# A Conformer-style layer on one core: weight differences on VectorE, and a new order at the start of both FFNs

## The chip, the core and the metric

The kernel runs on one core of a Trainium2 chip, as one launch. A core has TensorE (PE in the profile; its weight loads are PEld), VectorE (DVE), ScalarE (ACT), GpSimd (POOL) and SyncE (SP), each with an instruction queue of its own that it works through in order, and 16 DMA engines. The metric is the device time of the launch in microseconds; the median of several runs counts.

## The reference

One layer over x of 1024 tokens and 1024 channels, all in float32 (D_FF is 2816), and a final RMSNorm:

```python
x = x + 0.5 * _swiglu(_rmsnorm(x, ffn1_norm), ffn1_w_gate, ffn1_w_up, ffn1_w_down)
h = _rmsnorm(x, mix_norm); z = h @ w_in
y_a = _spatial_gating(gelu(z[..., :1024]), ...)      # gMLP, 4 groups
y_b = _mlstm_mixer(z[..., 1024:], ...)               # mLSTM, 4 heads
x = x + concat([y_a, y_b]) @ w_out
x = x + 0.5 * _swiglu(_rmsnorm(x, ffn2_norm), ffn2_w_gate, ffn2_w_up, ffn2_w_down)
out = _rmsnorm(x, final_norm)
# _swiglu(x, g, u, d) = (silu(x @ g) * (x @ u)) @ d
```

## The kernel before

**Layout.** x is held transposed, in two chunks c of 512 tokens, each as eight tiles of 128 channels by 512 tokens. Every matmul that needs float32 accuracy is made of three faster ones: an operand is split in a rounded part hi (a cast on ACT, L198) and a rest lo (a subtraction on DVE, L201), and `mm3` (L132) sums hi x hi, hi x lo and lo x hi.

**Seven products instead of eight.** Both FFN matrix products are done by Strassen's scheme in Winograd's form over 2 x 2 blocks, with seven products M = 1 to 7. The activation side has seven units A11, A12, A22, S1, S2, S3, S4 (`A_OF`, L47), which `h_units` (L213) makes: `first` normalizes chunk 0 and splits A11 and A12, `second` normalizes chunk 1 and makes S1, S2, S4, S3 and A22 in turn. That is 16 DVE instructions for S1 (eight normalizations, four sums, four splits), 8 each for S2, S4 and S3, 4 for A22. The weight side has four products (M = 5, 6, 7, 4) whose weight is a difference of two blocks; the difference is made in place in the raw tile and then split into a unit of one of two rings of four.

**gate_up (L255)** goes over 22 blocks b (gate and up weights of 11 pairs), seven products each. One product is four k tiles times three matmuls, twelve, into a PSUM bank; chains X (M = 1, 6, 7, 4), Z (5, 3) and W (2) share banks. The steps begin with the first three blocks interleaved: M = 1 and M = 2 of blocks 0, 1, 2 (steps 0 to 5), then M = 5, 6, 3, 7, 4 of blocks 0 and 1 (steps 6 to 15), then block 2. The difference (L282 to L291) is on DVE for blocks 0 and 1 and on POOL for the others.

**run (L371)** is the loop over steps: it calls `product(i)`, evacuates, then prepares `weight(i + ahead)`, ahead = 6 in gate_up and 3 in down. With `first=6` the first six evacuations are held back until after product 5, and `then()` (the whole of `second`) is issued ahead of them and ahead of weight 11. In FFN2, `then` is `later2`, which first computes the RMS statistics of chunk 1 (`rstd`, L152: a cast, a subtraction, two matmuls with a matrix of ones, then `rsqrt` with a logarithm and an exponential on ACT and four DVE instructions) and then calls `second`.

**down (L396)** goes product by product (M in the order 2, 1, 5, 6, 3, 7, 4), 11 pairs p each; one step is a split of the streamed activation (au<-as) and of the weight (wu<-wq), and 12 matmuls. `diff` (L433) makes the weight differences on POOL five steps ahead, `fetch` issues the loads eight steps ahead on SP's queue. When a chain ends, `evac` (L470) adds into x (L476) and calls a hook: in FFN1 and in the mixer the hook stores x to DRAM on SP's queue and adds its square to an accumulator; at the end of FFN2, `tail3` squares and accumulates on ACT and DVE, multiplies x by the final norm's gain on ACT (L976), and, once a chunk is complete, computes the statistics, multiplies by them on DVE and, for every third tile, POOL (L982), and stores.

A list scheduler places each engine's instructions when the program is built: the order in the code is the priority, and an instruction whose inputs it takes to be ready may go ahead of one that is not. On the chip each queue then runs in that fixed order.

Of the kernel before, what the change touches and what calls it, by code (L numbers as in the profile page):

```python
# [10 lines left out]
F32 = mybir.dt.float32  # L11
F32R = mybir.dt.float32r
AF = mybir.ActivationFunctionType
# [9 lines left out]
KT = D // P  # L23
# [23 lines left out]
A_OF = {1: "A11", 2: "A12", 3: "S4", 4: "A22", 5: "S1", 6: "S2", 7: "S3"}  # L47
UNITS = ("A11", "A12", "A22", "S1", "S2", "S3", "S4")
GROUPS = ((0, 4), (4, 8), (8, 11))


class Net:
# [97 lines left out]
        return acc  # L150

    def rstd(self, acc, hl, pst, pin=True):  # L152
        nc = self.nc
        hi, lo = hl[:, 0], hl[:, 1]
        nc.scalar.copy(hi, acc)
        nc.vector.tensor_sub(lo, acc, hi.bitcast(F32))
        ps = pst("stat")
        for i, a in enumerate((hi, lo)):
            ins = nc.tensor.matmul(ps, self.ones, a, start=i == 0, stop=i == 1)
            if i == 0 and pin:  # L160
                self.tc.keep_in_program_order(ins)
        return self.rsqrt(ps)

    def squares(self, c):
        nc = self.nc
# [47 lines left out]
    def h_units(self, gcol, r):  # L213
        nc = self.nc
        self.h = {
            u: tuple(self.big.tile([P, 4, T], F32R, tag="b", name=f"{u}{s}") for s in ("h", "l")) for u in UNITS
        }

        def put(u, k, src, eng=None):
            self.split(self.h[u][0][:, k], self.h[u][1][:, k], src, eng)  # L220

        def norm(c, k):
            x = self.x[c][k]
            g = self.cols[:, gcol + k : gcol + k + 1]
            nc.vector.scalar_tensor_tensor(x, x, g, r[c], op0=ALU.mult, op1=ALU.mult)
            return x

        def first():
            for j, u in enumerate(("A11", "A12")):
                for k in range(4):  # L230
                    put(u, k, norm(0, 4 * j + k))

        def second():
            x = self.x
            quads = [(x[0][k], x[0][4 + k], x[1][k], x[1][4 + k]) for k in range(4)]
            for k, (a11, a12, a21, a22) in enumerate(quads):
                norm(1, k)
                norm(1, 4 + k)
                nc.vector.tensor_add(a21, a21, a22)
                put("S1", k, a21)  # L240
            for k, (a11, a12, a21, a22) in enumerate(quads):
                nc.vector.tensor_sub(a21, a21, a11)
                put("S2", k, a21)
            for k, (a11, a12, a21, a22) in enumerate(quads):
                nc.vector.tensor_sub(a12, a12, a21)
                put("S4", k, a12)
            for k, (a11, a12, a21, a22) in enumerate(quads):
                nc.vector.tensor_sub(a21, a22, a21)
                put("S3", k, a21)
            for k, (a11, a12, a21, a22) in enumerate(quads):  # L250
                put("A22", k, a22)

        return first, second

    def gate_up(self, n):  # L255
        nc, d = self.nc, self.d
# [15 lines left out]

        def weight(b, M):
            r0 = row(b, 0)
            eng = nc.vector if b < early - 1 else nc.gpsimd
            if M in (1, 2):
                src = r0[:, M - 1]
            else:
                r1 = row(b, 1)
                if M == 5:  # L280
                    src = r1[:, 0]
                    eng.tensor_sub(src, r1[:, 0], r0[:, 0])  # L282
                elif M == 6:
                    src = r1[:, 0]
                    eng.tensor_sub(src, r1[:, 1], r1[:, 0])  # L285
                elif M == 7:
                    src = r0[:, 0]
                    eng.tensor_sub(src, r1[:, 0], r0[:, 0])
                elif M == 4:
                    src = r0[:, 1]  # L290
                    eng.tensor_sub(src, r0[:, 1], r1[:, 0])  # L291
                else:
                    src = r1[:, 1]
            w = self.unit("wu")
            name = self.split(w[:, 0], w[:, 1], src, after=fence.get("early"))
            if (b, M) == (early - 1, 2):
                fence["early"] = name
            return w
# [69 lines left out]
        steps.append((len(blocks) - 1, 4))  # L368
        return steps, weight, product, evac

    def run(self, steps, weight, product, evac, ahead, first=0, then=None, at=(), early=()):  # L371
        ready = {}
        n = len(steps)
        for what, lead in early:
            for i in range(min(lead, n)):
                what(*steps[i])
        for i in range(min(ahead, n)):
            ready[i] = weight(*steps[i])
        for i, (b, M) in enumerate(steps):
            for what, lead in early:  # L380
                if i + lead < n:
                    what(*steps[i + lead])
            product(b, M, ready.pop(i))
            if i >= first:
                evac(b, M)
            elif i == first - 1:
                then()
                for step in steps[:first]:
                    evac(*step)
            if i + ahead < len(steps):  # L390
                ready[i + ahead] = weight(*steps[i + ahead])
            for when, what in at:
                if when == (b, M):
                    what()

    def down(self, n, xsrc, hook, order, early=None):  # L396
# [36 lines left out]
        def diff(M, p):  # L433
            src = part(p, *source[M])
            if M == 5:
                nc.gpsimd.tensor_sub(src, src, part(p, 0, 0))
            elif M == 6:
                nc.gpsimd.tensor_sub(src, part(p, 1, 1), src)
            elif M == 7:
                nc.gpsimd.tensor_sub(src, part(p, 0, 1), src)  # L440
            elif M == 4:
                nc.gpsimd.tensor_sub(src, src, part(p, 0, 1))

        def units(M, p):
            a = self.unit("au", "u")
# [63 lines left out]
    def weight(self, key, ahead):  # L509
        at = next(i for i, (k, _) in enumerate(self.wq) if k == key)  # L510
        self.prepare(at + 1 + ahead)
        return self.wready[key]
# [376 lines left out]
def layer(ctx, tc, d):  # L889
# [17 lines left out]
    with ExitStack() as f1:  # L907
        net.ffn_pools(f1)
        net.load_x(d["x"])
        r[0] = net.rsqrt(net.squares(0))  # L910
        ps = net.squares(1)
        first, second = net.h_units(0, r)
        first()
        r[1] = net.rsqrt(ps)
        net.run(*net.gate_up(1), ahead=6, first=6, then=second)

        accs = [None, None]
        count = [0, 0]
        h = [None, None]

        def tail(c, k):
            nc.sync.dma_start(x1[c, :, k], net.x[c][k])
            accs[c] = net.square(net.x[c][k], accs[c], net.tmp)
            count[c] += 1
            if c == 0 and count[c] == KT:
                r[0] = net.rstd(accs[0], net.unit("sp"), net.fpsum)

        def early():
            h[0] = net.norm(0, 8, r[0], net.last_mm)

        net.down(1, d["x"], tail, order, ((4, 5), early))

    with ExitStack() as m:
        net.mix_pools(m)
        net.plan_mix()

        def stats1():
            r[1] = net.rstd(accs[1], mixhl(), mixst)

        def rest1():  # L940
            h[1] = net.norm(1, 8, r[1])

        accs2 = [None, None]

        def tail2(c, k):
            nc.sync.dma_start(x2[c, :, k], net.x[c][k])
            accs2[c] = net.square(net.x[c][k], accs2[c], mixsq)

        r2 = [None, None]
        h2 = []  # L950

        def nstats(c):
            r2[c] = net.rstd(accs2[c], mixhl(), mixst)

        def nrest(c):
            h2.extend(net.h_units(16, r2))
            h2[0]()

        net.mix(h, x1, stats1, rest1, tail2, nstats, nrest)

    with ExitStack() as f2:
        net.ffn_pools(f2)

        def later2():
            r2[1] = net.rstd(accs2[1], net.unit("sp"), net.fpsum, False)
            h2[1]()

        net.run(*net.gate_up(2), ahead=6, first=6, then=later2)

        accs3 = [None, None]  # L970
        count3 = [0, 0]

        def tail3(c, k):
            x = net.x[c][k]
            accs3[c] = net.square(x, accs3[c], net.tmp)
            nc.scalar.activation(x, x, AF.Copy, scale=net.cols[:, 24 + k : 25 + k])  # L976
            count3[c] += 1
            if count3[c] == KT:
                rf = net.rstd(accs3[c], net.unit("sp"), net.fpsum)
                for j in range(KT):  # L980
                    o = net.x[c][j]
                    (nc.gpsimd if j % 3 == 2 else nc.vector).tensor_mul(o, o, rf)  # L982
                    (nc.sync if j % 2 else nc.scalar).dma_start(d["out"][c, :, j], o)

        net.down(2, x2, tail3, order)

# [52 lines left out]
```

## Time and profile before

| | |
|---|---|
| median of 3 runs | 1748.37 us (1746.34 to 1748.84) |
| the profiled execution | 1748.65 us, span 1746.9 us |
| mean granted TensorE clock | 0.98 |
| PE busy in the span | 1662.6 us |
| DVE busy | 1108.7 us |
| ACT busy | 688.5 us |
| POOL busy | 447.8 us |

The stages by time in the span: FFN1 from 0 (gate_up to about 450 us, down to about 690), the mixer to 1057, FFN2 to the end (gate_up to about 1496, down to 1727, then the tail). The span goes from the first to the last instruction of the profiled execution; the time of the launch is 1.75 us longer. A row of a timeline gives start and duration in us, the engine and source line, the tile written and the tiles read, and how many alike were merged; in brackets stands how long the engine had been idle and who ended it. The hardware profiler models the ends of matmuls, so two matmuls in a row overlap in the records, and a few records can be missing.

### The profile page before, as it was taken

How to read it: one execution, taken by the hardware profiler on the slowest of the kernel's cores; microseconds unless marked ns; L12 is line 12 of the kernel's file. 1: busy time of each engine (PE TensorE's matmuls, PEld its weight loads, DVE VectorE, ACT ScalarE, POOL GpSimd, SP SyncE). 2: the span in 40 equal slices, each digit the busy share in tenths (PEclk: the TensorE clock that was granted, in tenths of full speed). 3: DMA queues.
4: the chain of work that ended last, by engine and by line, in shares of the span. 5: the costliest groups of instructions: out<-in, count | busy, mean ns of one | idle time of the engine just before them, and what ended most of it. 6: DMA issues, size and time to landing. Idle time of an engine off the chain costs nothing. (4 is left out here: it accounts for less than half of the span.)

```text
span 1746.9 us, 20121 instructions
## 1 busy us (share of the span) xinstructions
PE 1662.6 (95%) x7306; PEld 1347.8 (77%) x7306; DVE 1108.7 (63%) x1524; ACT 688.5 (39%) x1172; POOL 447.8 (26%) x331
## 2 busy tenths in 40 slices
PE   6799999999998999999999997999999999998995
PEld 3678888888886777888877885788888888876874
DVE  7965555555579767842636438955555554589575
ACT  5533333333443345531333324533333333443463
POOL 0133223222139200200304100222332322069000
PEclk9899999999999999999999998999999999999998
DMA  4242332332794232230310433233233331971331
GB/s 157 66 137 94 103 103 97 107 102 88 252 326 139 90 132 72 74 92 12 103 39 12 142 104 115 74 108 103 98 108 113 111 103 62 348 258 67 109 114 49
DMA packets 95701, 200.10 MB, mean 115 GB/s; under 512 B 10473, under 2 KB 14569, under 8 KB 95601
## 3 DMA queue, kind: packets, MB, share of 16 engines
q1 hardware_dynamic: 93712, 195.60, 33.4%
q10 hardware_dynamic: 1888, 3.21, 0.5%
q8 instruction: 57, 0.93, 0.2%
q14 instruction: 44, 0.35, 0.1%
HBM read 145.78 MB, written 52.99 MB: 114 GB/s over the span
## 5 line engine op out<-in xcount | busy, mean ns | idle before, releaser
L201 DVE TENSOR_TENSOR wu<-rg,wu 128x512 fp32r<-128x512 f32 x154 | 133.0, 865 | 128.8 <-ACT wu L198 127.6
L201 DVE TENSOR_TENSOR au<-as,au 128x512 fp32r<-128x512 f32 x154 | 144.5, 939 | 110.0 <-ACT au L198 109.2
L201 DVE TENSOR_TENSOR wu<-ru,wu 128x512 fp32r<-128x512 f32 x154 | 132.9, 864 | 85.7 <-ACT wu L198 84.7
L198 ACT CAST au<-as 128x512 fp32r<-128x512 f32 x154 | 95.7, 622 | 223.5 <-PE pX L138 117.3
L198 ACT CAST wu<-ru 128x512 fp32r<-128x512 f32 x154 | 95.9, 623 | 174.5 <-PE pX L138 53.9
L201 DVE TENSOR_TENSOR wu<-wq,wu 128x512 fp32r<-128x512 f32 x154 | 141.0, 918 | 6.0 <-ACT wu L198 5.9
L138 PE MATMUL pX<-au,wu 128*128 128x512 f32 x352 | 138.6, 394 | 5.6 <-DVE wu L201 5.6
L198 ACT CAST wu<-rg 128x512 fp32r<-128x512 f32 x154 | 95.3, 621 | 109.1 <-PE pZ L138 30.4
L136 PE MATMUL pX<-au,wu 128*128 128x512 f32 x352 | 137.7, 391 | 0.0
L137 PE MATMUL pX<-au,wu 128*128 128x512 f32 x352 | 137.7, 391 | 0.0
L198 ACT CAST wu<-wq 128x512 fp32r<-128x512 f32 x154 | 94.3, 615 | 9.3 <-PE pX L138 4.2
L282 POOL TENSOR_TENSOR rg<-rg,rg 128x512 f32<-128x512 f32 x20 | 26.5, 1326 | 247.7 <-DMA rg<-g 160.2
L138 PEld LDWEIGHTS pX<-au,wu 128*128 128x128 f32 x352 | 66.5, 189 | 22.7 <-DVE wu L201 9.0
L138 PE MATMUL pZ<-au,wu 128*128 128x512 f32 x176 | 71.5, 407 | 9.8 <-DVE wu L201 9.6
L138 PE MATMUL pZ<-S4h,wu 128*128 128x512 f32 x176 | 70.2, 399 | 8.5 <-DVE wu L201 8.5
L136 PE MATMUL pZ<-S1h,wu 128*128 128x512 f32 x176 | 68.9, 397 | 9.7 <-ACT S1h L198 9.6
L136 PEld LDWEIGHTS pX<-au,wu 128*128 128x128 f32 x352 | 66.5, 189 | 14.3 <-ACT wu L198 0.7
L137 PEld LDWEIGHTS pX<-au,wu 128*128 128x128 f32 x352 | 66.4, 189 | 13.8
L285 POOL TENSOR_TENSOR rg<-rg 128x512 f32<-128x512 f32 x20 | 33.1, 1653 | 170.6 <-DVE wu L201 140.8
L136 PE MATMUL pX<-A11h,wu 128*128 128x512 f32 x176 | 69.9, 398 | 5.2 <-ACT wu L198 2.9
L138 PE MATMUL pX<-A11h,wu 128*128 128x512 f32 x176 | 70.4, 401 | 4.1 <-DVE wu L201 4.1
L285 POOL TENSOR_TENSOR ru<-ru 128x512 f32<-128x512 f32 x20 | 26.6, 1331 | 179.3 <-DVE wu L201 179.3
(260 smaller groups left out, 4503.5 us busy)
## 6 DMA issues: line engine op xcount, KB each, us to landing
x<-x SPq DMA_DIRECT2D x96, 256.0 KB, 5.0
rg<-g SPq DMA_DIRECT2D x44, 512.0 KB, 3.6
ru<-u SPq DMA_DIRECT2D x44, 512.0 KB, 3.6
wq<-d SPq DMA_DIRECT2D x88, 256.0 KB, 5.3
as<-act1S SPq DMA_DIRECT2D x44, 256.0 KB, 3.1
as<-act2S SPq DMA_DIRECT2D x44, 256.0 KB, 3.4
act1S<-S SPq DMA_DIRECT2D x33, 256.0 KB, 2.1
as<-act1A SPq DMA_DIRECT2D x33, 256.0 KB, 4.3
```

The source lines that it names most:

```text
L136: nc.tensor.matmul(out, wh, hh, start=start and i == 0, stop=False, skip_group_check=True)
L137: nc.tensor.matmul(out, wh, hl, start=False, stop=False, skip_group_check=True)
L138: ins = nc.tensor.matmul(out, wl, hh, start=False, stop=stop and i == n - 1, skip_group_check=True)
L198: cast = nc.scalar.copy(hi, src)
L201: (eng or nc.vector).tensor_sub(lo, src, hi.bitcast(F32))
L282: eng.tensor_sub(src, r1[:, 0], r0[:, 0])
L285: eng.tensor_sub(src, r1[:, 1], r1[:, 0])
```

## The change

All weight differences of gate_up and down go to DVE. `second` is cut into five parts (S1, S2, S4, S3, A22), which `run` calls after steps 5, 5, 6, 8 and 9, each behind the weight prepared in that step; the six held evacuations follow after step 6. In FFN2 the accumulated squares of chunk 1 are split before the loop, and their two matmuls and `rsqrt` come with step 1. The x stores of FFN1 and of the mixer are issued from ACT's queue. At the end of FFN2 the gain and the statistics are applied by one DVE instruction per tile, POOL has no part in it, and for the last four tiles (chunk 1, k under 4) each square goes straight into a float32 matmul with ones, behind one for the sum of the first four, in place of accumulating, splitting and two matmuls.

```diff
+STAGES = (5, 5, 6, 8, 9)
     def rstd(self, acc, hl, pst, pin=True):
+        return self.rsqrt(self.total(self.hi_lo(acc, hl), pst, pin))
...
-        return first, second
+        return first, (s1, s2, s4, s3, a22)
...
-            eng = nc.vector if b < early - 1 else nc.gpsimd
...
-                    eng.tensor_sub(src, r1[:, 0], r0[:, 0])
+                    nc.vector.tensor_sub(src, r1[:, 0], r0[:, 0])
...
-    def run(self, steps, weight, product, evac, ahead, first=0, then=None, at=(), early=()):
+    def run(self, steps, weight, product, evac, ahead, hold=0, stages=(), at=(), early=()):
+        held = []
...
             product(b, M, ready.pop(i))
-            if i >= first:
+            if i < hold:
+                held.append((b, M))
+            else:
                 evac(b, M)
-            elif i == first - 1:
-                then()
-                for step in steps[:first]:
-                    evac(*step)
             if i + ahead < len(steps):
                 ready[i + ahead] = weight(*steps[i + ahead])
+            for when, what in stages:
+                if when == i:
+                    what()
+            if i == hold:
+                for step in held:
+                    evac(*step)
...
-                nc.gpsimd.tensor_sub(src, src, part(p, 0, 0))
+                nc.vector.tensor_sub(src, src, part(p, 0, 0))
...
-        net.run(*net.gate_up(1), ahead=6, first=6, then=second)
+        net.run(*net.gate_up(1), ahead=6, hold=6, stages=list(zip(STAGES, kinds)))
...
-            nc.sync.dma_start(x1[c, :, k], net.x[c][k])
+            nc.scalar.dma_start(x1[c, :, k], net.x[c][k])
...
-            nc.sync.dma_start(x2[c, :, k], net.x[c][k])
+            nc.scalar.dma_start(x2[c, :, k], net.x[c][k])
...
+        sums = net.hi_lo(accs2[1], net.unit("sp"))
+        def stats2():
+            r2[1] = net.rsqrt(net.total(sums, net.fpsum, False))
+        stages = [(1, stats2)] + list(zip(STAGES, h2[1]))
+        net.run(*net.gate_up(2), ahead=6, hold=6, stages=stages)
...
+        def output(c, ps):
+            rf = net.rsqrt(ps)
+            for j in range(KT):
+                o = net.x[c][j]
+                nc.vector.scalar_tensor_tensor(o, o, net.cols[:, 24 + j : 25 + j], rf, op0=ALU.mult, op1=ALU.mult)
+                (nc.sync if j % 2 else nc.scalar).dma_start(d["out"][c, :, j], o)
...
-            accs3[c] = net.square(x, accs3[c], net.tmp)
-            nc.scalar.activation(x, x, AF.Copy, scale=net.cols[:, 24 + k : 25 + k])
             count3[c] += 1
+            if c == 0 or k >= 4:
+                accs3[c] = net.square(x, accs3[c], net.tmp)
+                if count3[c] == KT:
+                    output(c, net.total(net.hi_lo(accs3[c], net.unit("sp")), net.fpsum))
+                return
+            ones = net.ones.bitcast(F32)
+            if count3[c] == 5:
+                last["ps"] = net.fpsum("stat")
+                nc.tensor.matmul(last["ps"], ones, accs3[c], start=True, stop=False)
+            sq = net.unit("sq").bitcast(F32)[:, 0]
+            nc.scalar.activation(sq, x, AF.Square)
+            nc.tensor.matmul(last["ps"], ones, sq, start=False, stop=count3[c] == KT)
             if count3[c] == KT:
-                rf = net.rstd(accs3[c], net.unit("sp"), net.fpsum)
-                for j in range(KT):
-                    o = net.x[c][j]
-                    (nc.gpsimd if j % 3 == 2 else nc.vector).tensor_mul(o, o, rf)
-                    (nc.sync if j % 2 else nc.scalar).dma_start(d["out"][c, :, j], o)
+                output(c, last["ps"])
```

## Rows read from the trace of the kernel before

**Rows 1.** The page: the span, and busy time by engine.

```profile
span 1746.9 us, 20121 instructions
...
PE 1662.6 (95%) x7306; PEld 1347.8 (77%) x7306; DVE 1108.7 (63%) x1524; ACT 688.5 (39%) x1172; POOL 447.8 (26%) x331
```

**Rows 2.** Windows: stretch, length, busy us by engine (instructions), PE clock, DMA share, GB/s.

```profile
61.00:100.00 39.00, 27.91 (x105) 21.78 (x104) 36.71 (x47) 19.04 (x32) 14.94 (x9) 0.82 0.42 136
100.00:505.00 405.00, 405.00 (x1788) 335.10 (x1787) 225.65 (x304) 152.16 (x259) 105.10 (x73) 1.00 0.39 133
526.00:580.00 54.00, 45.72 (x182) 34.13 (x181) 54.00 (x41) 19.47 (x35) 51.42 (x32) 0.97 0.36 118
...
1057.00:1079.00 22.00, 18.89 (x76) 14.76 (x74) 17.07 (x28) 9.41 (x17) 0.00 (x0) 0.92 0.42 141
1079.00:1127.00 48.00, 36.34 (x137) 27.79 (x137) 46.70 (x70) 26.50 (x46) 7.82 (x6) 0.82 0.21 65
1550.00:1618.00 68.00, 60.24 (x244) 45.91 (x243) 67.70 (x53) 27.84 (x49) 60.23 (x37) 0.97 0.35 119
1660.00:1725.00 65.00, 63.21 (x271) 51.56 (x270) 43.35 (x66) 34.02 (x59) 3.50 (x2) 0.97 0.23 77
```

**Rows 3.** Groups by line, 543 to 580 us (busy us, mean ns).

```profile
L201 DVE TENSOR_TENSOR au<-as,au 128x512 fp32r<-128x512 f32 x12 | 20.2, 1683 | 0.0
...
L438 POOL TENSOR_TENSOR wq<-wq 128x512 f32<-128x512 f32 x7 | 12.2, 1743 | 0.0
```

**Rows 4.** Groups by line, 582 to 622 us.

```profile
L201 DVE TENSOR_TENSOR au<-as,au 128x512 fp32r<-128x512 f32 x16 | 11.1, 691 | 17.8 <-ACT au L198 17.6
```

**Rows 5.** Timeline of PE in FFN1's start: product 11 resumes.

```profile
70.03 0.79 PE L138 MATMUL pZ<-S4h,wu 128*128 128x512 f32 x1 [8.54 <-DVE wu L201]
```

**Rows 6.** Timeline of DVE in FFN1's start: first S1 sum, last A22, weight 11.

```profile
41.84 0.68 DVE L239 TENSOR_TENSOR x<-x,x 128x512 f32<-128x512 f32 x1
...
66.30 1.29 DVE L201 TENSOR_TENSOR A22l<-x,A22h 128x512 fp32r<-128x512 f32 x2
...
69.30 0.68 DVE L201 TENSOR_TENSOR wu<-ru,wu 128x512 fp32r<-128x512 f32 x1
```

**Rows 7.** Timeline of PE in FFN2's start: product 6 begins.

```profile
1088.85 0.79 PE L136 MATMUL pZ<-S1h,wu 128*128 128x512 f32 x1 [9.62 <-ACT S1h L198]
```

**Rows 8.** Timeline of DVE in FFN2's start.

```profile
1059.09 1.49 DVE L149 TENSOR_TENSOR acc<-sq,acc 128x512 f32<-128x512 f32 x2
...
1064.30 0.69 DVE L201 TENSOR_TENSOR wu<-ru,wu 128x512 fp32r<-128x512 f32 x1 [3.12 <-ACT wu L198]
...
1084.44 3.10 DVE L225 SCALAR_TENSOR_TENSOR x<-x,cols,rstd 128x512 f32<-128x512 f32 x3
```

**Rows 9.** Timeline of ACT's queue: two DMA issues.

```profile
1680.23 0.85 ACTq L983 DMA_DIRECT2D out<-x  x2
```

**Rows 10.** Timeline of PE: FFN2's first product.

```profile
1060.25 0.50 PE L136 MATMUL pX<-A11h,wu 128*128 128x512 f32 x1 [2.94 <-ACT wu L198]
```

**Rows 11.** Timeline of the tail.

```profile
1725.11 2.05 DVE L476 SCALAR_TENSOR_TENSOR x<-pX,x 128x512 f32<-128x512 f32 x3 [6.89 <-PE pX L138]
...
1730.82 0.62 ACT L155 CAST sp<-acc 128x512 fp32r<-128x512 f32 x1
...
1731.49 1.52 PE L159 MATMUL stat<-sp,ones 128*128 128x512 f32 x2 [4.38 <-ACT sp L155]
...
1737.13 5.83 DVE L982 TENSOR_TENSOR x<-x,rstd 128x512 f32<-128x512 f32 x6
```

**Rows 12.** Timeline of PE: float32 matmuls with ones, three records.

```profile
12.91 1.45 PE L174 MATMUL stat<-sq,ones 128*128 128x512 f32 x3
```

**Rows 13.** Line 174 by itself: duration ns min/median/max.

```profile
L174 PE MATMUL stat<-sq,ones x16: 592/657/1221, 8.5 to 19.8; 128*128 128x512 f32 x16
```

**Rows 14.** Groups by line, whole span: POOL's idle time before the M = 5 difference.

```profile
L282 POOL TENSOR_TENSOR rg<-rg,rg 128x512 f32<-128x512 f32 x20 | 26.5, 1326 | 247.7 <-DMA rg<-g 160.2 <-ACT rstd L126 87.5
```

## What the trace says of the change: a prediction

> **What bounds the kernel now.** The page comes first: TensorE (PE) is busy 1662.6 of 1746.9 us, VectorE (DVE) 63%, GpSimd (POOL) 26% [rows 1]. A busy share over the whole span says little about a kernel with stages, so the table of windows comes next [rows 2]. From 100 to 505 us PE makes 1788 matmuls in 405 us, 0.2265 us each, without a gap; that pace is the measure for every other stretch. A product of three times four matmuls (twelve) so takes 2.72 us. What a stretch loses is its length less its matmuls times 0.2265:
>
> - 61 to 100, end of FFN1's start: 39.0 - 105 x 0.2265 = 15.2 us
> - 526 to 580, FFN1's down projection: 54.0 - 182 x 0.2265 = 12.8 us
> - 1057 to 1127, FFN2's start: 70.0 - 213 x 0.2265 = 21.8 us
> - 1550 to 1618, FFN2's down projection: 68.0 - 244 x 0.2265 = 12.7 us
> - 1660 to 1725, where chunk 0 is put out: 65.0 - 271 x 0.2265 = 3.6 us
>
> Behind the last matmul come 20 us of tail. In all the losing windows but the last DVE is busy 91 to 100% of the time; it feeds PE there.
>
> Why it is short of time differs. In the down projection the groups by line show each DVE subtraction of an "au" tile at 1683 ns on average while POOL works through its own subtractions at 1743 ns each; from 582 to 622 us, with POOL idle, the same instruction takes 691 ns [rows 3, 4]. Two such per product are 3.4 us against PE's 2.72. In the starts POOL does little and DVE simply has too much queued: in FFN1 the twelfth product (number 11, counted from 0 as below) waits 8.54 us for one weight tile, whose subtraction starts at 69.30, behind all of S1, S2, S4, S3 and A22 [rows 5, 6]. In FFN2 PE stands 9.62 us for the first S1 tile, because the statistics of chunk 1 are asked for only after the sixth product [rows 7], although their sum was complete at 1060.6 [rows 8].
>
> **The change, part by part.** *Differences in the down projection (L436 to L442).* 88 instructions leave POOL, 44 in each FFN. On DVE one takes 0.69 us [rows 4]. A product then asks of DVE two splits and, in four of seven kinds, one difference: 3 x 0.69 = 2.07 us against 2.72, and the DVE instructions are no longer stretched. Each stage keeps a remainder for the evacuations and squares that come on top where a chain ends (four and four of 0.7 us, once in some eleven products, with units three products ahead = 8.2 us of cover): I keep 0.8 and 0.7 us of loss. Gain 12.0 + 12.0 us. If the cover is gone because a difference stands in DVE's queue waiting for its weight transfer, everything behind it (splits, evacuations) waits as well; the lower bound is half of the gain.
>
> *Differences in gate/up (L282 to L291).* 160 on POOL, 80 in each FFN, go to DVE. In the steady stretch DVE is busy 225.65 of 405 us [rows 2]; the 73 POOL instructions in it would add 73 x 0.69 = 50 us, making 68% even if nothing gets shorter. PE loses nothing there now, so the gain is nothing; the cover is 32% idle DVE and weights prepared six products (16.3 us) ahead. If it is gone, the price is in the rival that ends slower.
>
> *h blocks between weight preparations, FFN1.* DVE works without a pause from 41.84 to 67.59: 42 of the 44 h instructions (S1 16, S2, S4, S3 8 each, A22 4; two were done) in 25.75 us, 0.613 us each [rows 6]. In the new order DVE has to finish before S3 is complete: 38 of those, weight 11 (one split), weights 12, 13, 14 (two each) and the four held M2 evacuations, 49 x 0.613 = 30.0, so at 71.9. Product 12, which multiplies S3, ends three matmuls later, at 72.6. A22 with weight 15 needs six more, 75.5, in time for product 14. Products 13 to 19 follow at PE's pace: 72.6 + 7 x 2.72 = 91.6. Before, product 19 ended at about 100: 105 matmuls after 61 are what was left of 11 and all of 12 to 19 [rows 2]. That is 8.4; TensorE's granted clock averaged 0.82 there, and PE will still pause before product 12, so I take 1.0 off: 7.4 us. Bounds: 0, if the order of the queue shifts the same wait elsewhere, and 11, if PE is never short after product 12 and S3 comes earlier.
>
> *Statistics at FFN2's second product, and the h blocks there.* The sum is complete at 1060.6 and DVE then idles 3.12 us [rows 8], so the split of the sum costs nothing. From 1064.3 until S3 is complete DVE has: 5 splits of weights 1 to 5, 9 of weights 6 to 14, 7 differences, 4 of the reciprocal root, 40 of the h blocks, 4 evacuations: 69 x 0.613 = 42.3, with 1.5 for waits on ScalarE (ACT) 1108.1; product 12 ends at 1108.8. Of the 213 matmuls up to 1127, two are the statistics and 156 the first 13 products; 55 remain, 12.5 us: 1121.3. Gain 5.7, rounded up to 6, as the first h normalizations, 3.10 us for three beside a POOL instruction [rows 8], get their 0.7 us each back. Bounds 2 and 10 (10: the whole 9.62 us wait [rows 7] goes and nothing takes its place).
>
> *x stores on ACT's queue.* 16 stores in each of two places leave SP's queue, where the loads of the next stage stood behind them, and enter ACT's, each beside the square of the same x, which waits for the same evacuation. Two issues on ACT take 0.85 us [rows 9]. They cost where ACT's next cast is on PE's path: at FFN2's first product, which waited 2.94 us for ACT [rows 10], and likewise at the mixer's first block. Two issues each are 2 x 0.85 = 1.7 at most, 0 if the casts go first; I take -1.0. The loads gain nothing that PE can use, since they wait for buffers.
>
> *Shorter tail.* Now: first evacuation 1725.11, the cast of the sum 1730.82, two matmuls from 1731.49 to 1733.01, scaling from 1737.13 to 1742.96 [rows 11]. New: no scaled copies on ACT, no accumulation on DVE, no cast and split of the sum; instead five matmuls in float32. One such matmul is a pair of records (16 for eight calls); three records in a row took 1.45 us and the last of them 0.59, so they start 0.43 apart and a matmul takes 0.86 [rows 12, 13]. They can't begin before the last product's matmuls, about 1727.1, so end at 1727.1 + 5 x 0.86 + 0.2 = 1731.6, 1.4 earlier. Eight scalings on DVE at 0.685 (2.05 us for three of that kind) are 5.5 us in place of 5.83 beside POOL: 0.3. With 0.3 for a clock that stays up through the statistics, 2.0 us; bounds 1 and 3.5 (the first of the five runs earlier and the squares pace the rest).
>
> *The output of chunk 0* keeps its order, and its 3.6 us of loss stay.
>
> Sum: 12.0 + 12.0 + 7.4 + 6.0 - 1.0 + 2.0 = 38.4 us. The profiled execution took 1748.65 us (span 1746.9 and 1.75 around it), 0.28 over the median of the runs. 1748.65 - 38.4 = 1710.2, so **1710 us**.
>
> A rule speaks against the change. The Trainium skill, Perfetto Trace Analysis, Optimizing Scalar/DVE Operations: where DVE is saturated, moving work off it, even to GpSimd, may help, with the caution that the two share a read port. In this trace DVE is saturated (36.71 of 39 us) in the starts [rows 2], so there the rule would leave the differences on POOL; in the down projection the caution fits, 1683 against 691 ns. By the rule the sum would be that of rival A, by the rows the one above.
>
> **Rivals.** *A: DVE stays the bound of the starts.* The third block's four differences (weights 16, 17, 19, 21) now also stand on DVE, 4 x 0.613 = 2.5 us a start, and if waits on ACT between a difference, its cast and its split keep DVE from packing, the reordering only moves the wait. For it: DVE is busy 94% there. Against: those four come after S3, when the h blocks are done. With 2 us instead of 13.4 left of both starts: 1721.6.
>
> *B: DVE's queue stands in the down projection.* DVE takes its instructions in order; POOL waited for transfers without hurting anyone. At half of the 24 us: 1722. Against: DVE has 0.65 us to spare in every product.
>
> *C: the starts mend altogether.* If S1 and S2 are ready as PE comes to them and the clock doesn't fall, 11 and 10 us come back there instead of 7.4 and 6, and the tail reaches 3.5, with no loss on ACT: 1748.65 - 24 - 21 - 3.5 = 1700.
>
> *D, slower: rows of gate/up hold DVE up.* The difference for M5 needs a second row, and POOL has stood 160.2 us for such rows in 20 instructions, 8 us each [rows 14]. If DVE stood that long, its weights and evacuations would stand too. A block is 7 x 2.72 = 19.0 us, of which DVE has 32% free, 6.1 us; beyond a stand of 6.1 us a block PE loses the excess. At 8 us that is 1.9 x 40 = 76 us: 1786. Against: POOL's 8 us are mostly idle time, as the rows are asked for six weights ahead; and M4's difference, which frees the row's buffer, gets shorter by 1 us.
>
> **How the numbers follow.** Forecast 0.55, by itself 1703 to 1718; A 0.17, B 0.12, C 0.11, D 0.04, no change at all 0.01. The likeliest gives 1710. The range reaches to C below and past A and B above, to both halved at once less some: 1697 to 1727. A measurement of this kernel tells about 0.2% (3.5 us) from no change: faster 0.94, same 0.02, slower 0.04.
>
> **What would show it.** POOL's busy time falls from 448 to about 60 us, L201's mean on "au" and "wu<-wq" to 0.69, and PE makes its 12 matmuls in 2.72 us through both down projections. The 8.5 us wait for a weight in FFN1 and the 9.6 us one for S1 are gone; shorter waits for S3 tiles and for "wu" stand at products 8 to 12. In the tail the statistics end near 1.4 us earlier relative to the last product. Wrong would be: DVE idle behind "DMA rg<-g" or "DMA wq<-d" with PE waiting; a difference row on DVE above 1 us; a start that loses as much as before.

## The result, and the profile after

The changed kernel takes 1707.65 us (median of 4 runs, 1707.55 to 1708.28) against 1748.51 us before: a ratio of 0.977, interval 0.9753 to 0.9787. 1710 was forecast. The page and the windows (columns as in [rows 2]), on the stretches that answer to [rows 1, 2]:

```profile
span 1706.5 us, 19863 instructions
...
PE 1655.5 (97%) x7314; PEld 1345.9 (79%) x7314; DVE 1111.5 (65%) x1771; ACT 679.4 (40%) x1155; POOL 60.3 (4%) x79
```

```profile
61.00:94.00 33.00, 28.88 (x112) 22.28 (x111) 31.53 (x53) 17.83 (x31) 0.00 (x0) 0.90 0.47 151
94.00:500.00 406.00, 406.00 (x1792) 335.98 (x1791) 247.80 (x381) 153.85 (x261) 0.00 (x0) 1.00 0.39 134
516.00:566.00 50.00, 50.00 (x222) 41.42 (x221) 49.42 (x82) 22.63 (x40) 0.00 (x0) 1.00 0.49 170
...
1063.00:1103.00 40.00, 33.27 (x133) 23.76 (x132) 39.66 (x66) 24.15 (x43) 0.00 (x0) 1.00 0.18 60
1532.00:1596.00 64.00, 64.00 (x284) 53.01 (x283) 55.57 (x92) 29.75 (x52) 0.00 (x0) 1.00 0.41 132
```

POOL fell from 447.8 to 60.3 us. In these stretches of the two down projections (third and fifth row) PE now has no pause: 222 matmuls in 50 us, where [rows 2] show 182 in 54. Over the whole of each projection one wait is left, 1.2 and 1.4 us, at chunk 0's statistics. In the second row's stretch (gate/up to 457 us, then products of down whose weight is no difference) DVE rose from 56% to 61% (247.80 of 406) and PE still loses nothing.

To see where each microsecond went, the two traces were laid side by side matmul by matmul (7278 product matmuls in the records of each), and the difference of their starts read at the borders of the stages (the forecast's 6.0 for FFN2's start and -1.0 for the stores stand here with half of the -1.0 at the mixer and half at FFN2):

| stage | forecast | measured |
|---|---|---|
| FFN1's start | +7.4 | +5.4 |
| FFN1's down projection | +12.0 | +13.3 |
| mixer's first block | -0.5 | -3.5 |
| FFN2's first product and start | +5.5 | +7.8 |
| FFN2's down projection | +12.0 | +12.9 |
| output of chunk 0 | 0 | +2.0 |
| tail | +2.0 | +3.05 |
| elsewhere | 0 | -0.6 |
| sum | +38.4 | +40.4 |

**Down.** The groups by line, 520 to 620 us (busy us, mean ns, idle before), answer to [rows 3]: the splits take 0.69 us instead of 1.68, and a difference on DVE costs the same.

```profile
L209 DVE TENSOR_TENSOR au<-as,au 128x512 fp32r<-128x512 f32 x37 | 25.5, 688 | 21.0 <-ACT au L206 21.0
L209 DVE TENSOR_TENSOR wu<-wq,wu 128x512 fp32r<-128x512 f32 x37 | 25.2, 686 | 0.1
L462 DVE TENSOR_TENSOR wq<-wq 128x512 f32<-128x512 f32 x10 | 6.7, 685 | 0.0
```

**FFN1's start.** PE's waits, in place of the one of [rows 5], and DVE's queue ahead of the second:

```profile
67.79 1.15 PE L137 MATMUL pX<-S3h,wu 128*128 128x512 f32 x2 [2.01 <-ACT S3h L206]
...
77.41 0.50 PE L137 MATMUL pZ<-S1h,wu 128*128 128x512 f32 x1 [2.10 <-ACT wu L206]
```

```profile
71.82 0.68 DVE L209 TENSOR_TENSOR S3l<-x,S3h 128x512 fp32r<-128x512 f32 x1
...
73.63 1.88 DVE L209 TENSOR_TENSOR A22l<-x,A22h 128x512 fp32r<-128x512 f32 x3
75.44 0.68 DVE L354 TENSOR_TENSOR u<-pZ,u 128x512 f32<-128x512 f32 x1
76.04 0.67 DVE L299 TENSOR_TENSOR rg<-rg,rg 128x512 f32<-128x512 f32 x1
```

S3 is complete at 72.5 (71.9 in the prediction) and A22 at 75.5 (75.5). But PE then waits once more, for weight 16 (M = 5 of block 2), whose difference (L299) stands behind A22's splits; its cast and PE's first matmul come only after it. The granted clock is 0.51 from 78.1 to 81.6, the lower of the two levels (1.2 GHz): ten matmuls in 3.5 us instead of 2.3.

**FFN2's start.** The wait of [rows 7] is gone, the one of [rows 10] is 3.35 us; then six short waits, 0.4 to 1.2 us each, until the one for the same weight 16:

```profile
1045.68 0.50 PE L137 MATMUL pX<-A11h,wu 128*128 128x512 f32 x1 [3.35 <-ACT wu L206]
...
1087.14 0.73 PE L137 MATMUL pX<-S3h,wu 128*128 128x512 f32 x2 [0.83 <-ACT S3h L206]
...
1096.17 0.50 PE L137 MATMUL pZ<-S1h,wu 128*128 128x512 f32 x1 [2.59 <-ACT wu L206]
```

**Mixer's first block.** ACT's queue, with the stores in it:

```profile
672.25 0.33 ACTq L944 DMA_DIRECT2D x<-x  x1
672.62 0.63 ACT L149 ACTIVATE sq<-x 128x512 f32<-128x512 f32 x1
672.93 0.33 ACTq L944 DMA_DIRECT2D x<-x  x1
673.30 0.63 ACT L149 ACTIVATE sq<-x 128x512 f32<-128x512 f32 x1
673.84 1.98 ACT L527 CAST whi<-raw 128x1024 fp32r<-128x1024 f32 x2
```

Two casts of the mixer's weights, on which PE waits, come behind all four pairs of store and square (the last two pairs are shown). In the kernel before the first cast stood between the squares:

```profile
690.90 1.03 ACT L505 CAST whi<-raw 128x1024 fp32r<-128x1024 f32 x1
691.83 1.15 ACT L148 ACTIVATE sq<-x 128x512 f32<-128x512 f32 x2
```

PE's waits in the changed kernel, and the window behind them:

```profile
674.92 0.50 PE L137 MATMUL pg<-hh,whi 128*128 128x512 f32 x1 [2.75 <-ACT whi L527]
677.08 0.79 PE L139 MATMUL pg<-hh,wlo 128*128 128x512 f32 x1 [1.38 <-DVE wlo L528]
```

```profile
675.50:682.30 6.80, 5.42 (x13) 4.13 (x13) 3.35 (x4) 0.93 (x2) 0.00 (x0) 0.50 0.46 154
```

PE paused longer (1.08 and 1.26 us before), and the clock stood at its lower level for 6.8 us. Before, it was 1.00 there:

```profile
693.00:700.00 7.00, 6.03 (x26) 4.99 (x27) 3.91 (x5) 1.60 (x3) 0.00 (x0) 1.00 0.67 195
```

**Tail**, answering to [rows 11]:

```profile
1687.76 2.73 DVE L498 SCALAR_TENSOR_TENSOR x<-pX,x 128x512 f32<-128x512 f32 x4 [6.89 <-PE pX L139]
...
1689.60 1.02 PE L1017 MATMUL stat<-acc,ones 128*128 128x512 f32 x2
...
1690.45 3.60 PE L1020 MATMUL stat<-sq,ones 128*128 128x512 f32 x8
...
1698.11 5.39 DVE L1003 SCALAR_TENSOR_TENSOR x<-x,cols,rstd 128x512 f32<-128x512 f32 x8
```

From the first evacuation to the scaling it is 10.35 us, 12.02 before.

### The profile page after: what moved, and what is told of

It reads as the page before. It is cut to its first block, busy times and chain, and to the rows that moved or that the text cites. A ratio compares the mean times of both kernels' runs of the same rounds, so it can differ in the third digit from the quotient of the medians.

```text
span 1706.5 us, 19863 instructions
## 1 busy us (share of the span) xinstructions
PE 1655.5 (97%) x7314; PEld 1345.9 (79%) x7314; DVE 1111.5 (65%) x1771; ACT 679.4 (40%) x1155; POOL 60.3 (4%) x79
## 4 chain that ended last, share of the span: by engine, by line
PE 91%; DVE 7%; ACT 1%; DMA 0%; issue 0%; SPq 0%; DVEq 0%; ACTq 0%
PE pX L137 14%; PE pX L139 14%; PE pX L138 14%; PE pZ L138 7%; PE pZ L137 7%; PE pZ L139 7%; PE pW L139 3%; PE pW L138 3%; PE pW L137 3%; PE pg L139 3%; PE pg L137 3%; PE pg L138 3%; PE pt L583 2%; PE pt L582 2%; PE pt L584 2%; DVE x L233 1%
## 5 line engine op out<-in xcount | busy, mean ns | idle before, releaser
L209 DVE TENSOR_TENSOR au<-as,au 128x512 fp32r<-128x512 f32 x154 | 106.1, 689 | 107.7 <-ACT au L206 107.4
L209 DVE TENSOR_TENSOR wu<-rg,wu 128x512 fp32r<-128x512 f32 x154 | 106.1, 690 | 101.4 <-ACT wu L206 101.0
L209 DVE TENSOR_TENSOR wu<-ru,wu 128x512 fp32r<-128x512 f32 x154 | 105.7, 688 | 57.6 <-ACT wu L206 57.1
L209 DVE TENSOR_TENSOR wu<-wq,wu 128x512 fp32r<-128x512 f32 x154 | 105.2, 685 | 4.2 <-ACT wu L206 4.2
L138 PEld LDWEIGHTS pX<-au,wu 128*128 128x128 f32 x352 | 66.1, 188 | 13.6
L138 PE MATMUL pZ<-S1l,wu 128*128 128x512 f32 x176 | 69.3, 394 | 2.6 <-DVE S1l L209 2.5
L137 PE MATMUL pX<-S3h,wu 128*128 128x512 f32 x176 | 68.9, 395 | 2.8 <-ACT S3h L206 2.8
L138 PE MATMUL pX<-A11l,wu 128*128 128x512 f32 x176 | 70.3, 399 | 0.2 <-DVE A11l L209 0.2
L137 PE MATMUL pX<-S2h,wu 128*128 128x512 f32 x176 | 68.6, 390 | 1.9 <-ACT m L340 1.9
L137 PE MATMUL pX<-A22h,wu 128*128 128x512 f32 x176 | 69.7, 396 | 0.0
```

Source lines behind the costliest of these rows:

```text
L137: nc.tensor.matmul(out, wh, hh, start=start and i == 0, stop=False, skip_group_check=True)
L138: nc.tensor.matmul(out, wh, hl, start=False, stop=False, skip_group_check=True)
L209: (eng or nc.vector).tensor_sub(lo, src, hi.bitcast(F32))
```

## Experiments

The theory: each term of the table belongs to its own edit. DVE was slow in down because POOL worked beside it; the starts gained from the placement of the h blocks, the earlier statistics and the differences together; the stores on ACT cost at the mixer. The rivals: DVE's amount of work is the bound, so POOL should help it (A); POOL only delivered late; the terms shift from one stage to the next. Each run undoes or adds one thing in the changed kernel, unless said otherwise. Before was 1748.18, 1748.91 and 1748.10 us beside the three groups of four.

**e1: down's differences back on POOL.**

```diff
-                nc.vector.tensor_sub(src, src, part(p, 0, 0))
+                nc.gpsimd.tensor_sub(src, src, part(p, 0, 0))
```

(likewise for M = 6, 7, 4)

> The changed kernel with the 88 differences of the two down projections back on POOL, all else as changed. Theory (POOL's reads stretch DVE's two-input instructions): both down projections lose their 13.1 and 12.6 us again, DVE's splits there go back to about 1.7 us while POOL works, and the time is 1707.6 + 25 = 1733 us. Rival (the gain there came from the tail, the starts or the x stores acting on the down projection): 1707 to 1715.

Measured: 1736.22 us (1733.89 to 1737.46). Matmul by matmul, 13.5 us are lost in FFN1's down and 12.8 in FFN2's, 26.2 of the 28 us. The groups of its down projection, 520 to 620 us:

```profile
L209 DVE TENSOR_TENSOR au<-as,au 128x512 fp32r<-128x512 f32 x33 | 37.9, 1150 | 19.2 <-ACT au L206 19.1
...
L498 DVE SCALAR_TENSOR_TENSOR x<-pX,x 128x512 f32<-128x512 f32 x8 | 4.9, 678 | 0.0
L150 DVE TENSOR_TENSOR acc<-sq,acc 128x512 f32<-128x512 f32 x3 | 4.6, 1517 | 0.7 <-ACT sq L149 0.7
```

(The first and third read two SBUF tiles, the second one SBUF tile and PSUM.) Beside POOL the DVE instructions with two SBUF inputs lengthen, to 1150 and 1517 ns; the evacuation stays at 678. These means mix stretches with POOL busy and idle. From 522 to 559 us, where POOL is busy 36.45 of 37 us, the splits of a product take 1774 and 1650 ns, together more than its 2.72 us:

```profile
L209 DVE TENSOR_TENSOR au<-as,au 128x512 fp32r<-128x512 f32 x10 | 17.7, 1774 | 0.0
```

The Trainium skill, SBUF — State Buffer, Who interferes with whom, says this: a DVE instruction with two SBUF inputs contends with a GpSimd instruction that reads SBUF, one with at most one SBUF input doesn't, outside DVE's 2-port modes. The trace agrees: 1150 and 1517 ns against 678.

**e2 and e10: more work for POOL that nobody waits for.** One subtraction on POOL behind each of down's 88 differences, its result in a bf16 tile that nothing reads. e2 took 512 columns and, to make room, padded the temporaries' tiles by 8 columns instead of 16; e10 takes 384 columns and leaves the padding. Both add work that the layer doesn't need.

```diff
+            if M in (5, 6, 7, 4):
+                nc.gpsimd.tensor_sub(self.scratch, src[:, 0:384], part(p, 0, 1)[:, 0:384])
```

> The changed kernel, differences on DVE, and behind each of the 88 differences of the down projections one more POOL subtraction that reads the same weight tiles and writes a scratch tile that nobody reads (written in bfloat16, as there is no room for float32). It adds work that no part of the output needs. Contention theory: DVE's splits stretch from 0.69 to about 1.7 us beside POOL, PE loses some 8 to 13 us in each down projection: 1723 to 1733 us. Rival (what hurt was that POOL delivered the differences late, each 1.6 us and in POOL's own queue, and DVE is quick): nobody waits for these, so 1707 to 1709 us.

> One more subtraction of 384 columns on POOL behind each of the 88 differences of the two down projections; its result, a bf16 tile of its own, is used by nothing, and the padding of the other tiles stays as changed. DVE does all the differences. By the theory that POOL's busy time itself slows the path in down (through DVE, whose splits lengthen), 35 to 45 us are lost in down alone as in the run with 512 columns, scaled by 384/512: 1730 to 1742, and nothing elsewhere. By the rival, that POOL only delayed the weights' differences by its own length: 1707.6, within 2, since nothing waits for these.

e2: 1787.21 us; far more than expected, and 60 matmuls took 14.0 us instead of 13.6 even 300 us away from any POOL work. That was its padding (e9). e10: 1735.75 us (1733.87 to 1738.03), inside the expected times, though below the 35 to 45 us of loss named beside them: 28.2 us lost by the last matmul, 14.5 + 14.0 in the two down projections and under 0.6 anywhere else. Its groups, 520 to 620 us:

```profile
L467 POOL TENSOR_TENSOR scratch<-wq 128x384 bf16<-128x384 f32 x33 | 58.6, 1775 | 17.2 <-DVE wq L461 14.9
...
L139 PE MATMUL pZ<-au,wu 128*128 128x512 f32 x81 | 31.8, 392 | 2.1 <-DVE au L210 2.1
L210 DVE TENSOR_TENSOR wu<-wq,wu 128x512 fp32r<-128x512 f32 x33 | 30.3, 917 | 0.0
```

No engine waits for POOL in either down projection of this trace, yet the split goes from 686 to 917 ns and PE waits for it. That POOL delivered late is refuted as the cause there; its running beside DVE is enough.

**e9: the padding alone.**

```diff
-        return self.xt.tile([P, T + 16], F32, tag="t", name=name)[:, 0:n]
+        return self.xt.tile([P, T + 8], F32, tag="t", name=name)[:, 0:n]
```

> The changed kernel with one thing altered: the 512-wide tiles of the temporaries' pool are padded by 8 columns in place of 16, so that tiles behind them lie at other addresses; no work is added. In the run with the extra POOL subtractions this padding had changed too, and 60 matmuls took 14.0 us in place of 13.6 over the whole run, far from any POOL work. If the addresses did that: about 0.4 x 7278/60 = 48 us more, 1756 (1745 to 1760), with the pace of the steady stretches at 0.233. If the extra work did it in some way: 1707.6, within 2.

Measured: 1738.93 us (1738.02 to 1739.04), 31 us slower without one instruction more, and less than the 48 expected, because the down projections are spared. 29.7 us are lost by the last matmul: 9.7 in FFN1's steady gate/up stretch (120 matmuls take 28.0 us, not 27.2), 7.3 in the mixer, 10.0 in FFN2's steady part, the rest in the two starts, and none in either down projection. One matmul's row, 130 to 330 us, here and then in the changed kernel:

```profile
L137 PE MATMUL pX<-S3h,wu 128*128 128x512 f32 x44 | 17.4, 395 | 0.0
```

```profile
L137 PE MATMUL pX<-S3h,wu 128*128 128x512 f32 x44 | 17.1, 389 | 0.0
```

The clock is 1.00 in both and each matmul takes 6 ns more; only where the tiles lie was changed. The e2 trace against e9's: 24.7 us lost in FFN1's down, 24.3 in FFN2's, 0.0 in the steady stretches. Which operand's address matters was not tried.

**e3: gate/up differences of blocks 2 and on back on POOL**, as before, and as rival A's rule would have it.

```diff
+            eng = nc.vector if b < early - 1 else nc.gpsimd
-                    nc.vector.tensor_sub(src, r1[:, 0], r0[:, 0])
+                    eng.tensor_sub(src, r1[:, 0], r0[:, 0])
```

(likewise for M = 6, 7, 4)

> The changed kernel with the 160 gate/up differences of blocks 2 and up back on POOL. My theory: nothing in the steady stretch, where PE has no gap either way; in the starts the fourth of a microsecond either way per instruction, so 1707 to 1710 us. Rival (DVE is the bound of the starts, and four differences less on it free it): 2 to 2.5 us sooner in each start, 1703 us. A second rival (POOL in the steady stretch stretches DVE enough to cost PE): 1712 or more.

Measured: 1713.46 us (1712.84 to 1715.85): 2.5 us lost in FFN1's start, 3.1 in FFN2's, 0.0 in the steady stretches. The time is that of the second rival, the place is not, and the 1707 to 1710 of the theory were wrong. What the rule beside rival A would leave to POOL costs time even where DVE is busiest. POOL, DVE and ACT in FFN1's start:

```profile
69.34 5.11 POOL L300 TENSOR_TENSOR rg<-rg,rg 128x512 f32<-128x512 f32 x1 [67.69 <-DMA rg<-g]
...
72.03 1.28 DVE L209 TENSOR_TENSOR A22l<-x,A22h 128x512 fp32r<-128x512 f32 x2
...
74.48 0.62 ACT L206 CAST wu<-rg 128x512 fp32r<-128x512 f32 x1 [3.01 <-POOL rg L300]
```

The difference for weight 16 takes POOL 5.11 us instead of 1.28: it starts while DVE runs two-input instructions one behind the other, 0.68 us each, and ends 1.14 us after DVE stops. Here it is POOL that is slowed, and late: ACT stands 3.01 us for it.

**e5: all h blocks at step 5, ahead of the evacuations and weight 11. e6: FFN2's statistics at step 5.**

```diff
-STAGES = (5, 5, 6, 8, 9)
+STAGES = (5, 5, 5, 5, 5)
```

(e5 also moves the loop over the stages and, to step 5, the held evacuations ahead of `weight`, as in the kernel before.)

```diff
-        stages = [(1, stats2)] + list(zip(STAGES, h2[1]))
+        stages = [(5, stats2)] + list(zip(STAGES, h2[1]))
```

> All four h blocks stand at step 5 again, ahead of the evacuations of that step and of weight 11's preparation, as in the kernel before; the differences stay on DVE and all else stays as changed. The placement theory: the changed kernel gained 5.4 us at FFN1's start and 8.7 at FFN2's, and putting all differences of these starts back on POOL cost 5.8 in all, so placement (with the early statistics) carries the larger part; with every block at step 5 the four blocks' splits and norms delay evacuations and weights 11 and on, about 4 to 8 us in each start: 1715 to 1723. The rival, that the starts gained from the differences alone and the placement is of no account: 1707.6, within 2.

> FFN2's second statistics come at its fifth product again instead of its second; h blocks, differences, stores and tail stay as changed. The theory of the prediction: the chain of the statistics (the sum's matmuls, two ACT steps, four DVE steps) then ends some four products later, about 11 us, and S1, wanted 24 product steps after the start by the pair's order, is late by part of it: the wait of 9.6 us in front of the first block of sums comes back in part, 3 to 9 us, so 1711 to 1717. The rival, that the h blocks' own places set the start and the statistics have slack: 1707.6, within 1.5.

Measured: e5 1711.34 us (1710.85 to 1712.09), e6 1712.60 us (1711.96 to 1712.94). PE's timeline of e5, and then of e6:

```profile
70.51 0.79 PE L139 MATMUL pZ<-S4h,wu 128*128 128x512 f32 x1 [8.55 <-DVE wu L209]
```

```profile
1072.35 1.22 PE L137 MATMUL pZ<-S1h,wu 128*128 128x512 f32 x2 [8.00 <-ACT S1h L206]
```

In e5 the wait of [rows 5] is back in full, 8.55 us, but FFN1's start loses 0.7 us only: behind it PE no longer waits for S3 or weight 16. FFN2's start loses 3.1. So the placement mainly split one long wait into several. Its worth, 3.7 us in all, lies between the two expectations, 4 to 8 a start and nothing. In e6 the wait of [rows 7] is back, at 8.00 us, and costs 4.9 net: the early statistics carry most of FFN2's gain.

**e7: the old output section.** (Its ACT copies, POOL's share and the sum in high and low parts.)

> The output section of the kernel before for both chunks (scaling by the column on ACT, a third of the last products on POOL, sum of squares split in high and low parts), all else as changed. The ledger of the two traces gives 3.05 us after the last product and 2.0 us at the border between FFN2's third and fourth M, where chunk 0 is put out: if both belong to the tail's code, 1712.7 (1711.5 to 1713.5). The prediction's reading, that chunk 0's loss has nothing to do with how its output is written: 1710.7.

Measured: 1710.80 us (1710.07 to 1711.64). From the first evacuation (1687.16) to the scaling (1699.18) it is 12.02 us again, so the tail's 3 us are its code. At chunk 0's output only 0.4 us come back. The other 1.6 of before was the clock: in it PE made nine matmuls from 1672.0 to 1675.2 at 0.51, while e7 has 1.00 there with the same code. Why the clock fell in the one and not in the other stays open.

**e4: both x stores on SP. e8: only x1's, x2's on ACT.**

```diff
-            nc.scalar.dma_start(x1[c, :, k], net.x[c][k])
+            nc.sync.dma_start(x1[c, :, k], net.x[c][k])
```

> The changed kernel with the x stores of FFN1 and the mixer back on SP's queue. By the two traces the mixer's start lost 3.4 us and FFN2's first product about 0.9 against before. Theory (the stores on ACT pushed the first weight casts of the next stage behind all four squares): both come back, 1707.6 - 4.3 = 1703.3 us, and the mixer's first cast stands between the squares again. Rival (the loss comes from DVE's or the scheduler's other changes around the stage border): 1707 to 1708 us.

> Only the x1 stores go back to SP's queue; the x2 stores stay on ACT's. In the run with both stores on SP the mixer's start came back by 2.75 us, and about 3.7 us were lost around FFN2's start, where a weight load stood on SP's queue behind the last x2 stores and landed 3.5 us late. If each belongs to its own store: 1704.9 (1704 to 1706), faster than the changed kernel. The rival, that the gain at the mixer's start is given back at the next place whatever the x2 stores do: 1707.6 to 1709.

Measured: e4 1708.98 us (1707.83 to 1710.89), e8 1705.54 us (1705.14 to 1706.34). Neither expectation for e4 holds: the mixer's block gains 2.75 us back, but FFN2's first product and start lose 3.2. Its SP queue, and then ACT's:

```profile
1040.88 1.06 SPq L968 DMA_DIRECT2D x<-x  x2
1042.04 0.40 SPq L288 DMA_DIRECT2D ru<-u  x1
```

```profile
1047.84 0.62 ACT L206 CAST wu<-ru 128x512 fp32r<-128x512 f32 x1 [3.61 <-DMA ru<-u]
```

With x2 on SP the load of a weight row is issued behind the last two stores, at 1042.04 (1036.92 in the changed kernel), and ACT stands 3.61 us for it; FFN2's first product waits 4.52 us, 3.35 in the changed kernel. So x1's store belongs on SP and x2's on ACT, and e8 does that: 3.4 us back at the mixer, with ACT's queue and the window of the block:

```profile
671.38 1.03 ACT L527 CAST whi<-raw 128x1024 fp32r<-128x1024 f32 x1
```

```profile
673.00:680.00 7.00, 5.74 (x25) 4.60 (x25) 4.40 (x6) 2.02 (x3) 0.00 (x0) 1.00 0.58 189
```

The cast stands between the squares again, and the clock stays at 1.00. FFN2's start lost 1.5 us: behind the same wait for weight 16 (2.58 us, 2.59 in the changed kernel) the clock was 0.50 from 1093.4 to 1096.8, where it had stayed at 1.00. Why it fell stays open.

**e11 and e12: a step further, from e8.** A22 one step later, or S3 one step earlier.

```diff
-STAGES = (5, 5, 6, 8, 9)
+STAGES = (5, 5, 6, 8, 10)
```

(e12: 5, 5, 6, 7, 9; both with x1's stores on SP)

> x1 stores on SP, x2 stores on ACT, and A22's block one step later (step 10 in place of 9) in both FFNs, so that weight 16's preparation stands ahead of it on DVE. In the changed kernel PE waited 2.26 us (FFN1) and 2.75 us (FFN2) for weight 16, whose difference stood behind A22's four splits, with a half-clock stretch behind the first. If the order on DVE is the cause, these go: 1700 to 1703.5. If DVE's whole work is the bound, A22 is late in weight 16's place: 1705 to 1707.

> x1 stores on SP, x2 stores on ACT, and S3's block one step earlier (step 7 in place of 8) in both FFNs, ahead of weight 13's preparation on DVE. In the changed kernel PE waited 2.17 us (FFN1) and 0.99 us (FFN2) for S3. If the order on DVE is the cause: 1702 to 1704.5. If DVE's whole work is the bound, the wait moves to the weights behind it: 1705 to 1707.

Measured: e11 1701.58 us (1699.52 to 1702.18), e12 1708.68 us (1706.21 to 1711.00). PE's timeline in FFN2's start, e11, and in FFN1's, e12:

```profile
1088.58 0.50 PE L137 MATMUL pZ<-S1h,wu 128*128 128x512 f32 x1 [0.19 <-ACT wu L206]
```

```profile
77.92 0.50 PE L137 MATMUL pZ<-S1h,wu 128*128 128x512 f32 x1 [4.38 <-ACT wu L206]
```

In e11 the wait for weight 16 is 0.19 us where it was 2.59, and against e8 FFN1's start gains 2.3 us and FFN2's 2.8, with the clock at 1.00 behind both, where e8 had fallen to its lower level. That wait was DVE's order, not its amount of work. In e12 S3 comes earlier (PE waits 0.81 us for it, 1.99 in e8), but weight 16 pays: 4.38 us, 3.19 in e8. So the two waits cancel. The time is 3.1 us above e8's and above both expectations; of the 2.5 us between the two traces 1.1 stand ahead of the first product, where both kernels do the same, and the rest is not explained. e11 is the fastest version, at 0.973 of before (0.9714 to 0.9746).

## Why the prediction was right

- *Down, +12.0 each: 13.3 and 12.9.* The mechanism is shown from both sides: e1 brings the loss back, and e10 makes it with POOL work that nobody needs. The loss of 0.8 and 0.7 us kept for chain ends wasn't there; three units of cover held. Rival B is refuted: from 500 to 690 us DVE stood for a weight's transfer only twice, 1.5 us in all, and PE lost nothing by it.
- *Gate/up, 0.* Right: 406.00 of 406 us busy. Rival D is refuted by its size, not by its mechanism: from 94 to 457 us DVE did stand for rows, 16 times and 17.0 us in all, at most 1.5 at once, and PE never waited.
- *FFN1's start, +7.4: 5.4.* S3 and A22 came as worked out. The step that failed was "Products 13 to 19 follow at PE's pace": weight 16's difference, which now stands on DVE, came behind A22 (2.10 us of wait, then about 1.2 at the lower clock, 3.3 where 1.0 had been taken off for all of PE's pauses). That is rival A's place, but not its cause, as e11 shows; the remedy named beside A, POOL, made it worse (e3). The gain was also credited to the placement. Undone alone, placement costs 0.7 and the differences of later blocks 2.5, 3.2 of the 5.4 together; the rest shows in neither, and both undone at once was not run.
- *FFN2, +5.5: 7.8.* Mis-sized: S3 was complete at 1091.87, 1106.9 in the old trace's time (15.0 us behind at the mixer's end), where the prediction has 1108.1. That is 1.2 of the 2.3 us; the rest isn't traced. Statistics (4.9), placement (3.1) and differences (3.1) overlap: undone one by one they cost 11.1.
- *Stores on ACT, -1.0: -3.5 at the mixer; the -0.9 at FFN2's first product isn't shown to be theirs, since e4 without them is later there.* The mis-sized step is "Two issues each are 2 x 0.85 = 1.7 at most": the four stores changed the order on ACT, both casts fell behind all squares, and the clock fell. And "The loads gain nothing" was wrong for x2: without its stores on ACT, FFN2's start loses 3.2 us (e4).
- *Tail, +2.0: 3.05.* Five matmuls of 0.86 us were right (ten records in 4.45 us). From evacuation to scaling 1.67 us went instead of 1.4, by scaling without POOL 0.44 instead of 0.3, and 0.94 behind the scaling, where nothing was credited (the last stores land 2.1 us after issue, 2.6 before, by medians).
- *Chunk 0's output, 0: +2.0.* 0.4 is code, 1.6 the clock (e7).

The misses, -2.0, -3.0 and -0.6 against +1.3, +2.3, +0.9, +2.0 and +1.05, add up to 2.0; that the total came out nearer than its terms is luck.

## What to carry to other kernels

An engine that is off the path can still be on it through what it shares with a neighbour: look at whether the same instruction is longer while a neighbour works, and try work nobody waits for. Where several things on a queue are late, the order decides which wait you see, so trace each wait to what stands ahead of it and move only what isn't wanted yet. A transfer moved to another queue takes a place there: ask for each stage what it stands in front of.

## What the runs showed of the hardware

- Padding one pool's tiles by 8 columns instead of 16 (a row of 2080 bytes instead of 2112) made each matmul of gate/up and mixer slower, 395 ns instead of 389 in the records, 28.0 us instead of 27.2 for 120, and 31 us in all, at the same clock.
- DVE instructions with two SBUF inputs took 0.9 to 1.5 us on average in stretches with POOL at work (e1, e10), those with a PSUM input 0.68 as ever.
- A POOL subtraction with two SBUF inputs, started while DVE ran two-input instructions back to back, took 5.11 us instead of 1.28 and ended 1.14 us after DVE stopped (e3, one case).
- The same pause at the same place dropped the clock in one kernel and not in another: with waits of 1.08 and 1.26 us it stayed at 1.00 in e8 and fell to 0.63 on average from 675.5 to 680 in e4; with 2.75 and 1.38 in the changed kernel it was 0.50 for 6.8 us.
